# The list schedule's price of a matmul, set to other lengths

## The chip, the cores and the metric

One core of one Trainium2 chip runs the whole program. The metric is device time in microseconds (us) of one execution; lower is better. Engines: PE is TensorE, DVE is VectorE, ACT is ScalarE, POOL is GpSimd; SP issues the large loads.

## What is computed

Three transformer-like layers on one sequence of 512 tokens of width 1024, in float32. The first block mixes sparse top-k attention with a chunked state-space scan and then runs a two-of-sixteen mixture of experts. The second block runs twice; each time it does a hybrid mixer, a cross-attention to a memory of 256 rows and a SwiGLU:

```python
def first_block(x, ...):
    proj = x @ w_in                       # q, k, v, index heads, z, xbc, dt
    att  = dsa_attention(q, k, v, iq, ik, iw, topk)
    ssd  = ssd_mixer(z, xbc, dt_raw, ...)
    x = layer_norm(ALPHA * x + concat([att, ssd]) @ w_out)
    return layer_norm(ALPHA * x + hier_moe(x, ...))

def second_block(h, mem, ...):            # for each of two layers
    h = layer_norm(A2 * h + hybrid_mixer(h, ...))       # attention + RG-LRU
    h = layer_norm(A2 * h + cross_attention(h, mem, ...))
    return layer_norm(A2 * h + swiglu(h, wi, wo))       # widths 1024 -> 2816 -> 1024
```

## The kernel before, in words

**The arithmetic.** Every large product is made of three matmuls: each float32 operand is split into a high part and a low part of type float32r, and high x high, low x high and high x low are added in PSUM (`feat_mm` L850, `tok_mm` L860). The stationary tile has 128 x 128 elements, the moving one up to 512 columns. A piece of weights is loaded by SP as `raw`, cast by ACT to `wh`, and the rest `wl = raw - wh` is made by DVE, or by POOL for four keys, the first memory projection `ck0` among them (`Stream.take` L545, L572). Four pieces fit in the ring. A few small products in the state-space chunks (`ssd_chunk` L1098) and twelve warm-up matmuls are true four-byte float32 matmuls; BF16 appears in the routing alone.

**What sets the order.** Nothing is issued while the code is being read. `Plan.new` (L216) writes each instruction down with its operands, a price in ns and a priority, which is its place in the code. `Plan.run` (L349) then plays the program through: every engine is free or busy by the prices, an instruction becomes ready when the prices of what it needs have passed plus a latency between engines (`LAT`, L181), and a free engine takes the ready one that comes first in the code (`pick`, L413). The instruction is issued in that order, and on the chip each engine's queue keeps that order, whatever the real times are. A loaded tile must have a free slot before its first instruction may be taken (`held`, L399). Prices so touch neither the instructions nor their number, only their order on each queue.

**Where that leaves a choice.** In the wide products PE has one stream of ready matmuls and takes them in code order. In four stretches it has two: a chain of small steps between PE, DVE, ACT and POOL, and matmuls of low priority that cover the chain. They are the first block's chunks (`ssd_chunk`, `topk`, `attend`, L1262), covered by the memory projections `ck` and `cv` of the second block; the routing (`route` L1475), covered by more of `ck`; the experts (L1719); and the layer norms (`tok_phase` L1359, `norm_feat` L1301), covered by the first units of the next product (`feat_units` L1811). A chunk's chain ends in the inverse square root on DVE (`rsqrt` L1038, tiles `rs_y`), the scaling of `y` (L1163), and PE's transposes of `y` (L1166).

**The prices.** `Plan.add` (L306) sets them. For PE (L324 to L331) `n` is the number of output columns, `args[1]` the stationary tile and `args[2]` the moving one.

Of the kernel before, what the change touches and what calls it, by code (L numbers as in the profile page):

```python
# [14 lines left out]
BF16 = mybir.dt.bfloat16  # L15
# [177 lines left out]
class Plan:  # L193
# [112 lines left out]
    def add(self, eng, method, args, kw):  # L306
        if self.direct:
            f = lambda x: x.real() if isinstance(x, View) else x
            return getattr(eng.real, method)(*[f(x) for x in args], **{k: f(x) for k, x in kw.items()})
        views = [v for v in list(args) + list(kw.values()) if isinstance(v, View)]  # L310
        writes = [kw[k] for k in ("out", "accum_out") if isinstance(kw.get(k), View)]
        if args and "out" not in kw and isinstance(args[0], View):
            writes.append(args[0])
        reads = [v for v in views if not any(v is w for w in writes)]
        def fn():
            f = lambda x: x.real() if isinstance(x, View) else x
            return getattr(eng.real, method)(*[f(x) for x in args], **{k: f(x) for k, x in kw.items()})  # L317
        n = max([v.columns() for v in views if method in ("tensor_reduce", "max", "bn_stats") or v in writes] or [1])
        lat, table, nbytes = 0.0, None, 0
        if method == "dma_start":  # L320
            o = writes[0] if writes else reads[0]
            nbytes = o.columns() * 4 * (o.box[0][1] - o.box[0][0])
            cost = 1040.0 if eng.name == "Pool" else 60.0
        elif eng.name == "PE":  # L324
            n = writes[0].columns()
            if method == "transpose":
                cost = 109.0
            elif args[1].buf.dtype == F32:
                cost = max(216.0, 1.667 * n)
            else:  # L330
                cost = max(27.0 if args[2].buf.dtype == BF16 else 109.0, 0.4167 * n + 2.5)  # L331
        elif eng.name == "ACT":
            aps = sum(isinstance(kw.get(k), View) for k in ("bias", "scale"))
            cost = 0.836 * n + (50, 143, 235)[aps] + (0 if args[1].buf.pool.psum else 42) + (93 if "accum_out" in kw else 0)
            table = SETS.get(args[2].name)
        elif eng.name == "DVE":
            rate = 1.042
            if method in ("tensor_copy", "memset", "tensor_scalar") and not any(v.buf.pool.psum for v in views):
                rate = 0.6
            if method == "reciprocal":  # L340
                rate = 8.3
            cost = rate * n + 66 + 30 * sum(v.columns() == 1 for v in reads if n > 100)
        else:
            cost = 1.85 * n + 60
        op = self.new(eng.name, fn, cost, reads, writes, lat)
        op.table, op.bytes, op.name = table, nbytes, method
        return op
# [1934 lines left out]
```

## Time and profile before

| | us |
|---|---|
| median of 3 runs | 2419.61 (2418.84 to 2421.11) |
| the profiled execution, its own time | 2428.73 |
| its span, first to last instruction | 2426.9 |
| around the span | 1.83 |
| PE busy | 2365.1 (97%) |
| DVE, ACT, POOL busy | 1495.0, 1146.8, 359.1 |

A busy PE is not PE at its peak, since matmuls overlap in the records: their pace is read from the starts of a run of equal matmuls. The granted clock of TensorE has two levels; 1.00 in a window means the whole window at the upper one (2.4 GHz), 0.51 nearly all of it at the lower one (1.2 GHz).

### The profile page before, as it was taken

What the parts mean: (1) busy time and instruction counts of PE and PEld (TensorE: products, weight loads), DVE (VectorE), ACT (ScalarE), POOL (GpSimd) and SP (SyncE); (2) the same over time, 40 slices, a digit from 0 to 9 for tenths busy, and PEclk for the clock granted to TensorE, in tenths of its full rate; (3) what the DMA queues carried; (4) which work ended last, traced back from release to release, by engine and by line L of the source; (5) the groups of instructions that cost most, each with busy time, mean ns of one, the idle gap of its engine ahead of it and who ended that gap; (6) DMA issues with size and microseconds to landing.
All of it is one profiled execution on the core that took longest, in us unless ns stands there. A gap on an engine that the chain in (4) does not pass through costs nothing.

```text
span 2426.9 us, 30226 instructions
## 1 busy us (share of the span) xinstructions
PE 2365.1 (97%) x11681; PEld 1960.6 (81%) x11681; DVE 1495.0 (62%) x2591; ACT 1146.8 (47%) x2004; POOL 359.1 (15%) x261
## 2 busy tenths in 40 slices
PE   9999989989999999999999999999999999999998
PEld 8777877768888887888888888888887898888886
DVE  5977689986983668756333335794477756432334
ACT  5447458756762663545222235673474544322221
POOL 1462432211000004403000001000004303000000
PEclk9979999999999999999999999999999999999999
DMA  6222769984113334322222333113323322332322
GB/s 185 73 76 70 236 205 333 342 299 125 54 61 104 113 98 163 102 73 70 92 99 87 104 104 119 57 53 97 120 92 125 116 94 87 104 105 87 104 79 77
DMA packets 215426, 290.42 MB, mean 120 GB/s; under 512 B 10784, under 2 KB 166640, under 8 KB 214768
## 3 DMA queue, kind: packets, MB, share of 16 engines
q1 hardware_dynamic: 203888, 260.44, 33.0%
q0 software_dynamic: 11392, 28.02, 3.6%
q8 instruction: 92, 1.51, 0.3%
q14 instruction: 54, 0.44, 0.1%
HBM read 275.85 MB, written 20.97 MB: 122 GB/s over the span
## 4 chain that ended last, share of the span: by engine, by line
PE 76%; DVE 8%; ACT 2%; issue 1%; DMA 1%; DVEq 0%; POOL 0%; ACTq 0%; POOLq 0%
PE fu L317 10%; PE fg L317 10%; PE fo L317 10%; PE ps L317 6%; PE ba L317 4%; PE gn L317 4%; PE q L317 4%; PE xr L317 4%; PE gr L317 4%; PE ga L317 4%; PE co L317 3%; PE wo L317 3%; PE gu L317 2%; DVE hTl L317 2%; PE cq L317 2%; PE bn L317 2%
## 5 line engine op out<-in xcount | busy, mean ns | idle before, releaser
L317 DVE TENSOR_TENSOR wl<-raw,wh 128x1024 fp32r<-128x1024 f32 (+1 forms) x390 | 489.2, 1264 | 460.2 <-ACT wh L317 459.5
L317 ACT ACTIVATE wh<-raw 128x1024 fp32r<-128x1024 f32 (+1 forms) x414 | 433.8, 1057 | 551.7 <-PE fu L317 156.5
L317 POOL TENSOR_TENSOR htokL<-htokL,lngb 128x1024 f32<-128x1024 f32 x48 | 132.9, 2783 | 291.5 <-PE ps L317 288.4
L303 ACT ACTIVATE lntmp<-ps,lnc 128x128 f32<-128x128 f32 x224 | 85.3, 467 | 50.4 <-PE ps L317 38.0
L317 ACT ACTIVATE fsil<-fg 128x512 f32<-128x512 f32 x44 | 26.3, 598 | 160.1 <-PE fg L317 160.1
L317 DVE TENSOR_TENSOR fsil<-fsil,fu 128x512 f32<-128x512 f32 x44 | 30.3, 688 | 104.9 <-PE fu L317 103.4
L317 PE MATMUL fg<-hTh,wh 128*128 128x512 f32 (+1 forms) x384 | 88.2, 372 | 0.0
L317 PE MATMUL fu<-hTh,wh 128*128 128x512 f32 (+1 forms) x384 | 88.2, 372 | 0.0
L317 PE MATMUL fu<-hTl,wh 128*128 128x512 f32 (+1 forms) x384 | 88.1, 372 | 0.0
L317 PE MATMUL fg<-hTh,wl 128*128 128x512 f32 (+1 forms) x384 | 88.0, 372 | 0.0
L317 PE MATMUL fu<-hTh,wl 128*128 128x512 f32 (+1 forms) x384 | 88.0, 371 | 0.0
L317 PE MATMUL fg<-hTl,wh 128*128 128x512 f32 (+1 forms) x384 | 88.0, 371 | 0.0
L317 DVE TENSOR_TENSOR hTl<-lntmp,hTh 128x512 fp32r<-128x512 f32 x56 | 76.9, 1384 | 10.3 <-ACT hTh L317 10.2
L317 PEld LDWEIGHTS fu<-hTl,wh 128*128 128x128 f32 x384 | 68.3, 188 | 12.5
L317 PEld LDWEIGHTS fg<-hTh,wl 128*128 128x128 f32 x384 | 68.3, 188 | 12.4
L317 PEld LDWEIGHTS fg<-hTl,wh 128*128 128x128 f32 x384 | 68.3, 188 | 12.5
L317 PEld LDWEIGHTS fu<-hTh,wl 128*128 128x128 f32 x384 | 68.3, 188 | 12.5
L317 PEld LDWEIGHTS fu<-hTh,wh 128*128 128x128 f32 x384 | 68.3, 188 | 12.4
L317 PEld LDWEIGHTS fg<-hTh,wh 128*128 128x128 f32 x384 | 68.1, 188 | 12.4
L317 PE MATMUL gu<-wh,hTm 128*128 128x512 f32 x256 | 73.5, 398 | 1.2 <-DVE hl L317 1.0
L317 POOL TENSOR_TENSOR wl<-raw,wh 128x1024 fp32r<-128x1024 f32 x24 | 58.2, 2431 | 104.3 <-ACT wh L317 104.2
L317 ACT ACT_TABLE_LOAD x53 | 68.0, 1283 | 11.7 <-DVE c_mx L317 5.6
(605 smaller groups left out, 5781.6 us busy)
## 6 DMA issues: line engine op xcount, KB each, us to landing
raw<-in_w_in_dram SPq DMA_DIRECT2D x47, 1024.0 KB, 5.3
raw<-in_ffn_wi_dram SPq DMA_DIRECT2D x44, 1024.0 KB, 5.2
raw<-in_ffn_wo_dram SPq DMA_DIRECT2D x20, 1024.0 KB, 5.0
raw<-in_ckv_w_dram SPq DMA_DIRECT2D x15, 1024.0 KB, 5.4
raw<-in_w_out_dram SPq DMA_DIRECT2D x12, 1024.0 KB, 5.0
raw<-in_w_down_dram SPq DMA_DIRECT2D x8, 1024.0 KB, 7.6
raw<-in_w_br_attn_dram SPq DMA_DIRECT2D x8, 1024.0 KB, 5.0
raw<-in_w_br_rnn_dram SPq DMA_DIRECT2D x8, 1024.0 KB, 5.0
```

What stands on the lines that cost most here:

```text
L303: "ACT": (lambda: act.activation(out.real(), src.real(), AF.Identity, bias=bias.real(), scale=scale.real()), 0.836 * n + 235, 0.0)}
L317: return getattr(eng.real, method)(*[f(x) for x in args], **{k: f(x) for k, x in kw.items()})
```

## The change

Two prices of PE are set to other numbers. A matmul with a float32 stationary tile is reckoned at 1.2 ns a column, at least 112 ns, in place of 1.667 ns, at least 216 ns. Any other matmul gets 13.5 ns beside its columns in place of 2.5 ns. Transposes, latencies, loads and all prices of other engines stay.

```diff
             elif args[1].buf.dtype == F32:
-                cost = max(216.0, 1.667 * n)
+                cost = max(112.0, 1.2 * n)
             else:
-                cost = max(27.0 if args[2].buf.dtype == BF16 else 109.0, 0.4167 * n + 2.5)
+                cost = max(27.0 if args[2].buf.dtype == BF16 else 109.0, 0.4167 * n + 13.5)
```

In ns: 512 columns 215.9 before and 226.9 after; 460 columns 194.2 and 205.2; 256 columns 109.2 and 120.2; 128 columns 109 both times; float32 with 64 columns 216 and 112, with 128 columns 216 and 153.6, with 256 columns 426.8 and 307.2.

## Rows read from the trace of the kernel before

**Rows 1.** The page: busy time by engine, and the granted clock in 40 slices.
```profile
PE 2365.1 (97%) x11681; PEld 1960.6 (81%) x11681; DVE 1495.0 (62%) x2591; ACT 1146.8 (47%) x2004; POOL 359.1 (15%) x261
...
PEclk9979999999999999999999999999999999999999
```

**Rows 2.** Busy time by window: PE, PEld, DVE, ACT, POOL (instructions); clock, DMA share, GB/s.
```profile
140.00:181.00 41.00, 37.06 (x181) 29.07 (x181) 27.82 (x86) 18.10 (x55) 21.89 (x17) 0.67 0.19 63
181.00:285.00 104.00, 103.88 (x543) 82.50 (x542) 68.07 (x170) 59.19 (x112) 30.71 (x32) 1.00 0.47 148
285.00:345.00 60.00, 48.86 (x341) 42.90 (x340) 51.17 (x93) 33.37 (x70) 33.55 (x20) 0.94 0.60 195
345.00:520.00 175.00, 163.40 (x869) 131.98 (x868) 158.40 (x211) 129.26 (x176) 46.62 (x47) 0.99 0.92 311
...
560.00:2427.00 1867.00, 1842.26 (x8898) 1533.36 (x8896) 1045.44 (x1721) 811.51 (x1423) 168.70 (x100) 1.00 0.30 95
```

**Rows 3.** What PE waited for: us in total, times, longest us.
```profile
PE route L317 <- DVE hTl L317: 8.0, 3, 4.4
PE hidT L317 <- DVE sg L317: 5.8, 7, 1.2
PE ps L317 <- DVE htokL L317: 5.7, 4, 2.6
PE bn L317 <- DVE L0sg L317: 4.5, 1, 4.5
```

**Rows 4.** The chain that ended last, in order of time: start, us, what.
```profile
1128.89 2.88 PE fu L317 x24
...
1192.28 5.44 PE fu L317 x24
```

**Rows 5.** The tile ssd: durations in ns (min/median/max), first and last start.
```profile
L317 PE MATMUL ssd<-xdt,L x64: 221/275/476, 138.3 to 223.9; 128*128 128x64 f32 x64
```

**Rows 6.** PE in order of time, a chunk's four-byte matmuls.
```profile
198.20 1.10 PE L317 MATMUL ssd<-xdt,L 128*128 128x64 f32 x8
199.24 0.65 PE L317 MATMUL ssd<-xe,btk 128*64 128x256 f32 x2
```

**Rows 7.** Busy time of PE in matmuls of ck, in 141.2 to 157.2 and 303 to 338.
```profile
141.20:157.20 16.00, 9.74 (x57) 0.87 0.25 84
303.00:338.00 35.00, 18.38 (x126) 0.90 0.68 232
```

**Rows 8.** The same of cq before a layer norm's last transposes, and of fg.
```profile
996.00:1003.00 7.00, 5.03 (x40) 1.00 0.01 2
...
1118.00:1122.00 4.00, 3.11 (x24) 1.00 0.00 0
```

**Rows 9.** All engines in order of time, 150.6 to 157.3.
```profile
150.59 1.05 ACT L317 ACTIVATE wh<-raw 128x1024 fp32r<-128x1024 f32 x1
...
151.72 4.83 POOL L317 TENSOR_TENSOR wl<-raw,wh 128x1024 fp32r<-128x1024 f32 x2 [3.64 <-ACT wh L317]
151.76 1.09 ACT L317 ACTIVATE pth<-ps 128x512 fp32r<-128x512 f32 x2
151.89 2.25 DVE L317 SCALAR_TENSOR_TENSOR rs_y<-rs_e,rs_y 128x1 f32<-128x1 f32 x1
...
154.40 2.70 DVE L317 SCALAR_TENSOR_TENSOR y<-y,rs_y,nw 128x512 f32<-128x512 f32 x1
...
157.24 0.45 PE L317 MATMUL ssd<-ca,y 128*128 128x128 f32 x1 [2.69 <-DVE y L317]
```

**Rows 10.** The tile rs_y: durations in ns (min/median/max).
```profile
L317 DVE SCALAR_TENSOR_TENSOR rs_y<-rs_e,rs_y x12: 141/154/2248, 150.2 to 232.5; 128x1 f32<-128x1 f32 x12
...
L317 DVE SCALAR_TENSOR_TENSOR y<-y,rs_y,nw x4: 741/752/2698, 154.4 to 233.6; 128x512 f32<-128x512 f32 x4
```

**Rows 11.** Busy time by window again, around the fall of the clock.
```profile
157.30:181.00 23.70, 23.70 (x86) 16.82 (x87) 10.62 (x36) 7.88 (x23) 10.15 (x10) 0.51 0.14 45
181.00:235.00 54.00, 53.88 (x310) 41.38 (x309) 41.22 (x127) 36.24 (x79) 18.23 (x16) 1.00 0.21 72
```

## The prediction, made before the changed kernel was built

> **What bounds the kernel now.** I read the page first. PE is busy for 97% of the span and its clock is at the upper level in all but a few early slices [rows 1]. So the time is PE's work, which the change leaves alone, plus what PE loses to waits and to the lower clock. The windows say where that is [rows 2]. From 560 us to the end PE is busy for 1842.26 of 1867 us at clock 1.00: there the products stand one behind the other. The losses lie ahead of that: 140 to 181 us (clock 0.67), 285 to 345 us (PE idle for 11.1 of 60 us) and the experts from 345 to 520 us (idle for 11.6 of 175 us). The waits name the releasers [rows 3], and in these rows it is always DVE that is late: for the routing's transposed input, for the experts' hidden tile, for a layer norm, for a bank of `bn`.
>
> **Is the new price right?** 24 matmuls of 512 columns take 5.44 us on the chain, 226.7 ns each; 24 of 256 columns take 2.88 us, 120 ns each [rows 4]. The new 226.9 and 120.2 ns are these lengths; the old 215.9 and 109.2 ns were 5% and 9% short. The Trainium skill, "TensorE: Matmul & The Clock Gate", section "Back-to-back issue gap", gives N/2.4 + 2.5 ns for a warm 512-column matmul, about 216 ns, which is the old price. This trace disagrees by 11 ns; were the page right here, every cover below would be planned thinner than it really is by another 2.7 us in all, and the sum would come to -3.1 in place of -5.8.
>
> For the four-byte matmuls the price gets worse. The code asks for 32 products of 64 columns (eight heads, four chunks), and the trace has 64 records of them [rows 5], so one product is two records. Eight records, four products, take 1.04 us from the first start to the next tile's [rows 6], 260 ns each. The old price was 216, the new one is 112: the length of a record, not of a product. With 32 of these, twenty other products and the twelve of the warm-up, and the same work running on PE before and after, I cost this at nothing on PE; it makes the planner expect the end of a chunk's eight products 0.83 us too soon (8 x 104 ns), which can leave DVE waiting for them in the four chunks, beside PE's covering work.
>
> **What the change does, part by part.** It removes and adds no instruction and no transfer. It re-draws the order of every queue, PE's, DVE's, ACT's, POOL's and SP's.
>
> (a) Stretches with one ready stream, 560 us to the end. The order is that of the code at either price, and what covers DVE and ACT there is PE itself (1842 busy us against 1045 and 812). I cost it at 0. The wait for `bn` (4.5 us [rows 3], and its like in the second layer) stays: DVE is slow there while POOL scales the norm's rows, which no price knows of. Bounds: -2 to +2 us, under half of one `bn` wait, because a tie between two DVE instructions may fall the other way.
>
> (b) Experts, 345 to 520 us. The transfers are busy for 0.92 of it at 311 GB/s, the most of any window [rows 2]. A PE wait that went away would meet the weights' arrival. Cost 0; bounds -3 to +3 us, half of the hidden tile's 5.8 us [rows 3].
>
> (c) Thinner cover. While a chain runs through DVE, the planner fills PE with matmuls until, by its prices, the chain is back. Priced 11 ns short, the fill lasted longer on the chip than planned, and this hid some of DVE's lateness. At the right price it holds fewer matmuls and the same lateness shows by that much more. Counting the fills ahead of waits: 57 `ck` in 141.2 to 157.2 us (0.63 us) and 126 `ck` around the routing [rows 7], of which I take half, since the later ones follow the last long wait (0.69 us); 40 `cq` ahead of a layer norm's last transposes and 24 `fg` ahead of the next one [rows 8], once in each layer (0.88 and 0.53 us). Sum **+2.7 us**. Bounds 0 (no chain is late) and +5.4 us (each at the lower clock).
>
> (d) The stall at 157 us. DVE's chain for the first chunk meets two POOL subtractions that start at 151.72: one 128 x 1 instruction, begun 0.17 us later, takes 2.25 us where the median of twelve is 0.154, and the scaling of `y` takes 2.70 us where the median is 0.752 [rows 9, 10]. PE waits 2.69 us for it, and the clock is then at 0.51 for 23.7 us. PE starts 86 matmuls there, and 310 in the 54 us after it at clock 1.00 [rows 11]: at that pace 86 take 15.0 us, so 8.7 us are lost to the clock and gaps, **11.4 us** with the wait. The mix of widths differs, so this is an estimate. Whether the collision stays hangs on a margin of 0.17 us. ACT makes the `wh` that POOL subtracts from just ahead of two copies of 1.09 us together [rows 9]. With a ring slot freed 0.63 us later in the plan (57 x 11 ns) and the chunk's products ended 0.83 us sooner, the two may swap; POOL would start 1.09 us later and find the small instructions done. Bounds: -11.4 (all of it) to +11.4 us (a second one in another chunk; the old stays). I take the share of the wait that the blocked small instruction makes, 2.10 of 2.69 or 0.78, less a little for the scaling of `y`, which may still collide: three quarters, **-8.5 us**.
>
> (e) Routing, 285 to 345 us. Its waits (4.4 us the longest) are DVE's under POOL's norm rows; the order of DVE's critical steps is kept by priority. Beyond (c) 0; bounds -5 to +5 us, about the longest wait.
>
> Sum: +2.7 - 8.5 = **-5.8 us**. The profiled execution would go from 2428.73 to 2422.9 us; it stands 9.1 us (0.4%) above the median of the runs. Against the median the same sum gives **2413.8 us**, 0.24% faster. A measurement of this kernel can tell about 0.2%, 4.8 us, from no change, so the forecast lies close to that edge.
>
> **The rivals.**
>
> *No change that can be told* (2414.8 to 2424.5 us). For it: PE's work is 97% of the span, 1867 us of it have one order, and the two large terms have opposite signs. If the collision of (d) only moves (saving the 2.1 us of one blocked instruction, the clock falling all the same), the sum is +2.7 - 2.1 = +0.6, 2420.2 us. Against it: the order in the first 560 us is re-drawn as a whole, and there a single wait cost 11 us. That the change doesn't do what it says, since prices only matter where two instructions are ready together, also ends here.
>
> *Slower: a thin cover brings the clock down in another chunk.* The place is 181 to 285 us, where PE is now busy for 103.88 of 104 us at clock 1.00 with `ck` and `cv` as cover. The price of four-byte products there is too low and the cover is thinner, so transposes of `y` are queued ahead of cover that PE could have run. It decides from the point at which the granted clock falls after the wait: the wait itself is 2.7 us, the spell at the lower clock up to 8.7. With (c) and with the old stall in place: 2419.6 + 2.7 + 2.7 = 2425.0 us without the fall, 2433.7 us with all of it; in the middle 2429.4 us. For it: the waits are late DVE work, which a right price of PE does not make earlier. Against it: there the subtractions for `cv` are DVE's own, not POOL's, so DVE's small steps meet POOL less.
>
> *More than forecast.* All of (d) goes and the routing gains 5 us: -11.4 + 2.7 - 5 = -13.7, 2405.9 us. It is the low part of the forecast's case.
>
> **How the numbers follow.** Faster than 2414.8 us (the forecast, centre 2413.8, its own range 2403 to 2414.8): 0.39. No change that can be told: 0.31. Slower than 2424.5 us: 0.30. The range reaches down past the 2405.9 us of the best case by the 3 us that the experts may add, to 2403 us, and up into the slower rival to 2431 us, which leaves out its upper end. Cases of both signs hold the chance, so it is wide.
>
> **What would show it right or wrong.** (a): from the fence on, the same order of PE's units, the pace 5.44 us for 24, and `bn` waiting 4.5 us. (b): experts within 3 us of 175. (c): about 36 `cq` where 40 stand, and that wait longer by 0.4 us. (d): no `rs_y` above 1 us, and the clock of 140 to 181 us near 1.00; if the collision stands there unchanged, the forecast's main term is wrong. A clock under 0.9 in 181 to 285 us would be the slower rival. If the stretch after 560 us differs by more than 2 us, (a) is wrong, and prices matter where I hold that they don't.

## The result, and the profile after

| | before | changed |
|---|---|---|
| median of the runs, us | 2419.23 (2418.49 to 2421.11, 4 runs) | 2455.68 (2447.98 to 2456.2, 4 runs) |
| ratio | | 1.014, 95% interval 1.012 to 1.016 |
| profiled execution, its span | 2418.0 (a second profile of the same kernel) | 2453.6 |

The change costs 36 us, where the forecast was a gain of 6 with 2431 us as the upper end of its range. The spans are compared with a second profile of the kernel before, since the first [rows 1 to 11] is 9 us longer than that kernel's median: its granted clock stayed low for 24 us after the stall of [rows 9], and in the second for 3.5 us after the same stall.

The page of the changed kernel, busy time and clock, to be read against [rows 1]:

```profile
PE 2369.8 (97%) x11681; PEld 1960.4 (80%) x11681; DVE 1498.3 (61%) x2590; ACT 1147.7 (47%) x2005; POOL 351.1 (14%) x261
...
PEclk9989999999999999999999999999998999999999
```

PE has the same 11681 matmuls and still 97% of the span. The page hides a loss of this kind, because a busy PE at half clock counts as busy. Its hints are the two 8s in the row of the clock, in the third slice (the first block's chunks) and in the 31st, far behind the experts; the second profile of the kernel before has 9 in all forty slices.

DVE has one instruction less than in [rows 1] and ACT one more: prices move more than the order on each queue. `Plan.copy` (L282) gives a copy to ACT or DVE, whichever the plan has free first, and of the 32 copies `of` in the attention 18 are on ACT in place of 14. This does not explain the time of that stage: the run price_8_0 below has 24 of them on ACT, and its attention takes as long as before (126.1 us).

The windows of the changed kernel that answer to [rows 2]:

```profile
140.00:181.00 41.00, 36.60 (x216) 31.37 (x213) 31.01 (x91) 19.06 (x56) 26.12 (x20) 0.79 0.15 45
181.00:285.00 104.00, 101.36 (x534) 80.17 (x533) 68.98 (x170) 56.33 (x111) 28.42 (x30) 1.00 0.47 145
285.00:345.00 60.00, 47.03 (x282) 39.76 (x281) 46.57 (x82) 33.45 (x67) 35.85 (x18) 0.89 0.62 204
345.00:520.00 175.00, 162.88 (x907) 132.97 (x907) 157.74 (x222) 128.87 (x174) 41.30 (x46) 0.99 0.90 307
560.00:2427.00 1867.00, 1840.31 (x8896) 1528.10 (x8897) 1035.88 (x1697) 820.83 (x1446) 168.87 (x106) 0.99 0.29 95
```

Fixed windows hold other work in each kernel once they are shifted against each other. The better cut is by stage, from the first matmul of one tile to the first of another. Windows cut so, first of the second profile of the kernel before (from `xbc` to the first `ssd`, on to the first `kv`, and the attention from `ga` to `ba`), then of the changed kernel; columns as in [rows 2]:

```profile
35.10:126.60 91.50, 89.68 (x427) 71.39 (x425) 81.27 (x209) 45.89 (x78) 32.27 (x16) 1.00 0.26 81
126.60:537.60 411.00, 380.17 (x2130) 309.76 (x2128) 340.83 (x619) 262.36 (x447) 145.49 (x123) 0.98 0.67 229
...
603.70:729.80 126.10, 125.78 (x666) 103.76 (x665) 103.53 (x318) 84.03 (x219) 0.00 (x0) 1.00 0.20 63
```

```profile
35.00:130.30 95.30, 92.41 (x427) 73.77 (x425) 85.17 (x213) 45.85 (x78) 31.79 (x16) 0.98 0.25 78
130.30:555.30 425.00, 387.20 (x2131) 315.73 (x2129) 339.08 (x615) 261.48 (x441) 142.29 (x123) 0.96 0.65 219
...
622.70:750.80 128.10, 127.28 (x668) 103.72 (x667) 102.12 (x316) 84.31 (x221) 0.00 (x0) 1.00 0.20 62
```

Now the counts agree: 427 matmuls in both, 2130 and 2131, 666 and 668. The same work takes 3.8, 14.0 and 2.0 us more. Of the 14.0, half is idle PE (30.8 to 37.8 us) and half is busy time, at a clock of 0.96 in place of 0.98: 34.1 us at the lower level in place of 17.1. The largest spell is in the first block's chunks:

```profile
143.40:157.10 13.70, 13.70 (x65) 12.25 (x65) 10.68 (x42) 6.71 (x24) 7.99 (x6) 0.50 0.06 21
```

The attention stage stands once in each layer. Of its 2.0 us only 0.5 is idle PE; the rest is busy PE at a clock of 1.00 in both kernels, and what lengthens that part is not shown. With the `bn` stage of layer 1, which is 10.1 us longer up to the first `fg` (230.6 against 220.5), these come to 31.8 of the 35.6 us between the spans (3.8 + 14.0 + 2.0 + 1.9 + 10.1); the other stages add at most 1.3 each.

The waits of PE in the changed kernel, to be read against [rows 3]:

```profile
PE bn L317 <- DVE L1sg L317: 13.8, 1, 13.8
PE hidT L317 <- DVE sg L317: 10.3, 12, 1.8
PE ps L317 <- DVE htokb L317: 8.7, 3, 6.0
PE ps L317 <- DVE htokL L317: 6.8, 4, 2.9
PE kv L317 <- ACT hTh L317: 4.4, 2, 4.2
PE pos L317 <- DVE Moh L317: 4.1, 1, 4.1
PE bn L317 <- DVE L0sg L317: 3.7, 2, 3.0
```

The three routing waits of 8.0 us together are gone. In their place stand 8.7 for the first block's norm rows `htokb`, 4.1 for `pos`, and one of 13.8 in a place where the kernel before waits 4.5.

**The wait of 13.8 us.** DVE, POOL and one line of PE in order of time, changed kernel, layer 1's `bn` stage:

```profile
1863.62 0.69 DVE L317 TENSOR_TENSOR L1sg<-L1sg,L1m1t 128x512 f32<-128x512 f32 x1
...
1864.23 20.06 DVE L317 TENSOR_TENSOR wl<-raw,wh 128x1024 fp32r<-128x1024 f32 x1
...
1864.61 18.59 POOL L317 TENSOR_TENSOR htokL<-htokL,lngb 128x1024 f32<-128x1024 f32 x8
...
1884.21 0.67 DVE L317 SCALAR_TENSOR_TENSOR L1sg<-L1sg,bn 128x512 f32<-128x512 f32 x1
...
1885.03 1.19 PE L317 MATMUL bn<-L1yh,wh 128*128 128x512 f32 x2 [13.77 <-DVE L1sg L317]
```

One subtraction of DVE, otherwise 1.22 us, lasts 20.06, to the end of POOL's eight scalings, which meanwhile run undisturbed (18.59 / 8 = 2.32 us each). PE runs out of banks behind it, and the clock is at 0.50 from 1874.0 to 1891.1 us. In the kernel before, the same eight take 23.41 us, and DVE's instructions get their turn between them; those with both inputs in SBUF take 2.3 to 3.4 us each (layer 0 of its first profile; layer 1 is alike):

```profile
913.05 1.22 DVE L317 TENSOR_TENSOR wl<-raw,wh 128x1024 fp32r<-128x1024 f32 x1
...
913.81 23.41 POOL L317 TENSOR_TENSOR htokL<-htokL,lngb 128x1024 f32<-128x1024 f32 x8 [0.61 <-DMA lngb<-in_ln_g_dram]
...
917.01 2.91 DVE L317 TENSOR_TENSOR L0sg<-L0sg,L0m1t 128x512 f32<-128x512 f32 x1
```

**The wait of 6.0 us.** ACT, DVE and PE in order of time: the changed kernel, then the second profile of before, from the norm's statistics to PE's transposes.

```profile
286.04 0.21 DVE L317 BATCH_NORM_AGGREGATE lnmv<-ln 128x2 f32<-128x12 f32 x1
...
287.44 2.01 ACT L317 ACTIVATE wh<-raw 128x1024 fp32r<-128x1024 f32 x2 [18.93 <-DMA raw<-in_ckv_w_dram]
...
290.32 2.00 ACT L317 ACTIVATE wh<-raw 128x1024 fp32r<-128x1024 f32 x2 [0.88 <-DMA raw<-in_ckv_w_dram]
292.34 1.28 ACT L317 ACT_TABLE_LOAD   x1
293.63 0.29 ACT L317 ACTIVATE lnsd<-lnmv,eps 128x1 f32<-128x1 f32 x1
...
296.17 1.12 PE L317 MATMUL ps<-ca,htokb 128*128 128x128 f32 x4 [6.02 <-DVE htokb L317]
```

```profile
272.51 2.01 ACT L317 ACTIVATE wh<-raw 128x1024 fp32r<-128x1024 f32 x2 [19.37 <-DMA raw<-in_ckv_w_dram]
275.54 0.21 DVE L317 BATCH_NORM_AGGREGATE lnmv<-ln 128x2 f32<-128x12 f32 x1
275.96 2.01 ACT L317 ACTIVATE wh<-raw 128x1024 fp32r<-128x1024 f32 x2 [1.43 <-DMA raw<-in_ckv_w_dram]
...
279.28 0.29 ACT L317 ACTIVATE lnsd<-lnmv,eps 128x1 f32<-128x1 f32 x1
...
281.38 1.09 PE L317 MATMUL ps<-ca,htokb 128*128 128x128 f32 x8 [1.26 <-DVE htokb L317]
```

The root `lnsd` of the norm is queued on ACT behind four casts of weights, and the casts wait for a transfer. In the changed kernel the transfer lands 1.4 us after the statistics are ready (287.44 against 286.04); in the kernel before the first pair of casts runs 3 us ahead of them. From statistics to root it is 7.6 us in place of 3.7. The plan's order put the root there, and the landing, which no price of PE describes, made it late. It is not one execution's: in the four profiles with this order of the first block (the change and the runs after_rows_dve, after_later and new_price_first below) the root comes 6.9 to 7.8 us after the statistics and the wait is 5.4 to 6.2 us; in the four with the order of before (its two profiles, before_rows_dve and new_price_later) 3.7 to 4.0 us and 1.4 to 2.0 us.

### The profile page after: what moved, and what is told of

It is laid out like the page before. It is cut to its first block, busy times and chain, and to the rows that moved or that the text cites. A ratio compares the mean times of both kernels' runs of the same rounds, so it can differ in the third digit from the quotient of the medians.

```text
span 2453.6 us, 30245 instructions
## 1 busy us (share of the span) xinstructions
PE 2369.8 (97%) x11681; PEld 1960.4 (80%) x11681; DVE 1498.3 (61%) x2590; ACT 1147.7 (47%) x2005; POOL 351.1 (14%) x261
## 4 chain that ended last, share of the span: by engine, by line
PE 70%; DVE 7%; ACT 1%; issue 0%; DVEq 0%
PE fu L317 10%; PE fg L317 10%; PE fo L317 10%; PE ps L317 5%; PE ba L317 4%; PE gr L317 4%; PE gn L317 4%; PE xr L317 4%; PE cq L317 3%; PE q L317 3%; PE co L317 3%; PE wo L317 3%; PE ga L317 3%; PE bn L317 2%; PE gate L317 2%; DVE hTl L317 2%
## 5 line engine op out<-in xcount | busy, mean ns | idle before, releaser
L317 DVE TENSOR_TENSOR wl<-raw,wh 128x1024 fp32r<-128x1024 f32 (+1 forms) x390 | 500.5, 1294 | 472.9 <-ACT wh L317 471.3
L317 PEld LDWEIGHTS fg<-hTl,wh 128*128 128x128 f32 x384 | 68.4, 188 | 12.5
L317 PEld LDWEIGHTS fg<-hTh,wl 128*128 128x128 f32 x384 | 68.3, 188 | 12.5
L317 PEld LDWEIGHTS fu<-hTh,wl 128*128 128x128 f32 x384 | 68.3, 188 | 12.5
L317 PEld LDWEIGHTS fu<-hTh,wh 128*128 128x128 f32 x384 | 68.3, 188 | 12.5
```

## The experiments

Two theories went into the first runs. Theory A: any other price draws another order, and what DVE then meets on POOL (or ACT on a transfer) decides. Theory B: the dearer matmul makes every cover thinner, and the time grows with the price. The stages, in us, from the first matmul of one tile to the first of the next (columns: first `xbc` to first `ssd`; `ssd` to the first `kv`; attention of one layer; `bn` to `fg` in layers 0 and 1), each from the kernel's profiled execution:

| kernel | median | xbc-ssd | ssd-kv | attention | bn-fg 0 | bn-fg 1 |
|---|---|---|---|---|---|---|
| before, first profile | 2419.61 | 91.5 | 420.5 | 126.1 | 221.2 | 220.9 |
| before, second profile | 2423.16 | 91.4 | 411.1 | 126.1 | 220.4 | 220.5 |
| only_four_byte | 2416.67 | 91.5 | 411.6 | 126.2 | 221.4 | 220.8 |
| price_minus_8_5 | 2436.82 | 89.5 | 419.8 | 125.0 | 220.1 | 227.4 |
| price_3_5 | 2415.63 | 91.4 | 413.7 | 125.3 | 221.1 | 220.8 |
| price_8_0 | 2440.85 | 93.6 | 427.1 | 126.1 | 221.9 | 220.4 |
| price_12_5 | 2448.64 | 92.6 | 420.9 | 127.8 | 221.8 | 231.4 |
| only_13_5 | 2446.83 | 95.3 | 425.8 | 128.1 | 221.1 | 231.4 |
| the change | 2455.68 | 95.3 | 425.0 | 128.0 | 221.1 | 230.6 |
| price_24_5 | 2476.94 | 101.2 | 427.2 | 131.4 | 222.7 | 223.0 |
| after_half_rows | 2450.81 | 95.2 | 429.5 | 128.1 | 217.9 | 231.4 |
| after_later | 2446.13 | 95.3 | 426.4 | 128.1 | 222.1 | 220.6 |
| late_400 | 2445.44 | 93.1 | 423.9 | 126.9 | 221.0 | 231.2 |
| new_price_first | 2437.54 | 94.4 | 428.0 | 126.1 | 221.0 | 221.0 |
| new_price_later | 2437.68 | 91.4 | 409.3 | 128.1 | 221.5 | 220.9 |
| after_rows_dve | 2433.75 | 94.2 | 428.5 | 128.0 | 215.4 | 215.4 |
| before_rows_dve | 2406.66 | 91.5 | 411.1 | 126.2 | 214.6 | 214.6 |
| four_rows_dve | 2406.1 | 91.5 | 406.8 | 126.2 | 214.7 | 214.8 |
| p3_5_rows_dve | 2401.35 | 91.4 | 411.7 | 125.2 | 214.8 | 213.3 |
| four_3_5_rows_dve | 2408.26 | 91.4 | 419.1 | 125.2 | 214.5 | 214.7 |

Each row of stages is one execution, and executions of one order differ. The four profiles with the first block's order of before have 91.4 to 91.5 and 409.3 to 420.5 us in the first two columns, the four with that of the change 94.2 to 95.3 and 425.0 to 428.5. So the order costs time in both stages, but a difference under some 11 us in `ssd-kv` between two single profiles can be the execution's.

**before_again**: the kernel before, unedited.

> The kernel before, once more, with a second profile. Its first profiled execution took 2428.7 us and its timed runs 2419.2. If single executions differ by where DVE's instructions fall among POOL's (both theories allow it), this profile is near 2419 and one of the three marked stretches is shorter: 140 to 181 us (clock 0.67 before) or the bn wait of layer 0 or 1 (4.5 us each, about 7 us with the clock). If the order alone fixes the time, the same stretches show the same losses within 1 us.

Measured: ratio 1.0004 (0.9989 to 1.0019), runs from 2419.75 to 2430.18 us. The stall of the first chunk is in this profile too:

```profile
154.37 2.26 DVE L317 SCALAR_TENSOR_TENSOR rs_y<-rs_e,rs_y 128x1 f32<-128x1 f32 x1
...
157.77 0.44 PE L317 MATMUL ssd<-ca,y 128*128 128x128 f32 x1 [3.88 <-DVE y L317]
```

```profile
157.00:160.50 3.50, 2.73 (x9) 2.38 (x10) 2.51 (x4) 0.60 (x1) 1.14 (x2) 0.53 0.69 167
140.00:181.00 41.00, 35.55 (x246) 29.77 (x245) 33.78 (x104) 24.76 (x70) 23.19 (x17) 0.96 0.24 77
```

The wait is 3.9 us, longer than the 2.7 of [rows 9], but the clock is low for 3.5 us only, and 140 to 181 us has 0.96 where [rows 2] show 0.67. So the long spell at the lower clock is not in every execution of the kernel. Two of these ten runs took some 2430 us and may hold it; no trace shows them.

**only_four_byte** and **only_13_5**: one price of the change each, the other left as it was.

```diff
-                cost = max(216.0, 1.667 * n)
+                cost = max(112.0, 1.2 * n)
```

```diff
-                cost = max(27.0 if args[2].buf.dtype == BF16 else 109.0, 0.4167 * n + 2.5)
+                cost = max(27.0 if args[2].buf.dtype == BF16 else 109.0, 0.4167 * n + 13.5)
```

> Only the price of the four-byte matmuls is changed (112 ns or 1.2 ns a column; the others keep 2.5 ns). Theory A (the order of the first 560 us is drawn anew by any change of a price, and what DVE's instructions then meet on POOL decides): off the 2419 us by several us either way, most likely 2415 to 2435. Theory B (thinner cover in proportion to the price): the four-byte price adds no cover and takes none, so 2419 within 4 us. If the four-byte price is the fault itself, about 2440 to 2455.

> Only the 13.5 ns in place of 2.5; the four-byte price as before. Theory A: some time between 2415 and 2460, with the front part (start of layer 0's first gate unit, 611.5 us before, 622.7 after) and the bn waits unlike both. Theory B: the whole of the loss, 2448 to 2456, with the front part near 622.

Measured: 0.9986 (0.9969 to 1.0003) and 1.0093 (1.0062 to 1.0125). The float32 price by itself costs nothing, as forecast; the 13.5 ns carry most of the loss. only_13_5's profiled execution, at 2458.33 us, has the same stages as the change, the held instruction in layer 1 (20.11 us) included. Its other four took 2444.27 to 2447.4 us, so its median is 9 us below the change's. That fits an instruction that is held in some executions only, but no trace of the shorter ones shows it, and whether the float32 price adds to the 13.5 ns stays open.

**after_half_rows**: the change, with POOL's scalings of rows cut into halves of 512 columns.

```diff
-            e.tensor_tensor(htok[t], htok[t], gb[0], op=OP.mult)
-            e.tensor_tensor(htok[t], htok[t], gb[1], op=OP.add)
+            for c in (slice(0, 512), slice(512, 1024)):
+                e.tensor_tensor(htok[t][:, c], htok[t][:, c], gb[0][:, c], op=OP.mult)
+                e.tensor_tensor(htok[t][:, c], htok[t][:, c], gb[1][:, c], op=OP.add)
```

> The changed kernel with POOL's scaling of the norm's rows cut into halves of 512 columns (same elements, twice as many instructions). Theory A: the one DVE subtraction of 20.06 us in layer 1's bn stage is a meeting of DVE with POOL's burst of eight; with other lengths the meeting falls otherwise, no DVE instruction there over 6 us, bn wait of layer 1 below 6 us in place of 13.9, time 2438 to 2448. Theory B (the order of the queues makes the bn wait): the order there is the same but for POOL, so the wait stays near 14 us and the time near 2455.

Measured: 1.0103 (1.007 to 1.0137), 2450.81 us. Layer 1 of this kernel, in order of time:

```profile
1864.31 21.25 DVE L317 TENSOR_TENSOR wl<-raw,wh 128x1024 fp32r<-128x1024 f32 x1
1864.77 19.69 POOL L317 TENSOR_TENSOR htokL<-htokL,lngb 128x512 f32<-128x512 f32 x16
```

Theory A had expected no instruction over 6 us there, and was wrong: sixteen instructions of half the length hold DVE as eight did. It is the burst that holds it, not one long instruction.

**price_minus_8_5, price_8_0, price_24_5**: other prices beside the columns, the old float32 price (`+ 2.5` becomes `- 8.5`, `+ 8.0`, `+ 24.5`).

> The price 0.4167 n - 8.5 ns (22 ns under the true length at 512 columns; 256 columns meet the floor of 109), four-byte price as before: covers planned thicker than before. Theory B (thin cover: the time grows with the price): 2405 to 2419, at or below the kernel before, with layer 0's first gate unit at or ahead of 604 us. Theory A (each price draws another order, and what DVE meets on POOL decides): not ordered by the price, anything from 2415 to 2460.

> The price 0.4167 n + 8.0 ns, half way between the two kernels, four-byte price as before. Theory B: half of the loss, 2428 to 2438, layer 0's first gate unit near 613. Theory A: not half way but in one place for each meeting: layer 1's bn wait either about 4.6 or about 14 us, nothing between, and the front part anywhere from 600 to 625.

> The price 0.4167 n + 24.5 ns, 11 ns over the true length, four-byte price as before: covers planned thinner still. Theory B: as far again beyond 13.5, 2465 to 2480, layer 0's first gate unit near 640. Theory A: no further growth with the price, 2420 to 2460.

Measured: 1.0061 (1.0032 to 1.009), 1.0072 (1.0045 to 1.0099) and 1.0216 (1.0179 to 1.0254). The old 2.5 ns is ahead of this lower price and of these higher ones. The table parts the two theories by stage. In `xbc-ssd` and the attention, theory B has the direction: 89.5 to 101.2 and 125.0 to 131.4 us from the lowest price to the highest, if not at every step. In `ssd-kv` the whole does not follow the price: 427.1 at 8.0 ns, 420.9 at 12.5, 427.2 at 24.5. Its idle PE does, roughly: 29.2 us at -8.5 ns, 30.8 at 2.5 (second profile), 31.8 at 8.0, 35.9 at 12.5, 37.1 in only_13_5 and 39.8 at 24.5. What scatters is the time at the lower clock: 17.1 us at 2.5 ns, 54.6 at 8.0, 30.7 at 12.5, 31.5 at 24.5. Of the 54.6 at 8.0 ns, 27.3 are one spell, like that of 24 us in the first profile of before. price_24_5's profile is of its shortest execution, 2464.93 us; the other three took 2476.16 to 2478.7.

**late_400**: the change, with 400 ns more planned latency from ACT and DVE to PE, which puts cover back.

```diff
-LAT = {"PEACT": 197, "PEDVE": 197, "PEPool": 222, "PEPE": 0, "ACTACT": 153, "ACTDVE": 142, "ACTPE": 271, "ACTPool": 180,
-       "DVEDVE": 127, "DVEACT": 128, "DVEPE": 202, "DVEPool": 153, "PoolPE": 203, "PoolPool": 120}
+LAT = {"PEACT": 197, "PEDVE": 197, "PEPool": 222, "PEPE": 0, "ACTACT": 153, "ACTDVE": 142, "ACTPE": 671, "ACTPool": 180,
+       "DVEDVE": 127, "DVEACT": 128, "DVEPE": 602, "DVEPool": 153, "PoolPE": 203, "PoolPool": 120}
```

> The changed kernel (13.5 ns and the four-byte price) with the planner's latency from ACT and from DVE to PE longer by 400 ns, so that covers are thick again although the price is true. Theory B: most of the front part's loss comes back: layer 0's first gate unit from 622.7 to 604 to 612, time 2425 to 2440 (the bn wait of layer 1 may stay). Theory A: no tie between the latency and the time, 2415 to 2460, with a bn wait of 4.6 or 14.

Measured: 1.0081 (1.005 to 1.0113). `xbc-ssd` falls from 95.3 to 93.1 us and the attention from 128.0 to 126.9 in each layer. So putting cover back returns 2.2 + 2 x 1.1 = 4.4 of the 7.7 us lost there, as thin cover asks for. Some 1 us of the 2.2 is within what the profiles of the change's order differ by. Of the whole, theory B had expected 2425 to 2440 us, and missed: `ssd-kv` (423.9, with 41.7 us of idle PE) and the held instruction (20.14 us) stay.

**after_rows_dve, before_rows_dve, four_rows_dve**: `load_rows` (L2096) scales on DVE, in the change, in the kernel before, and with the float32 price alone.

```diff
-                    norm_rows(t, gb, G)
+                    norm_rows(t, gb, V)
```

> The changed kernel, with the eight layer-norm scalings of load_rows in each layer moved from POOL to DVE, so that no burst of POOL runs beside the bn stage. Theory A (the loss in layer 1's bn stage is DVE held up by POOL's burst): no DVE operation there takes over 4 us, both stages from the first bn projection to wo come to 44 to 46 us (before: 51 to 52; changed: 50.6 and 61.5), and the run to 2432 to 2438 us, that is 2455 less 5 to 7 and less 15 to 17. Rival (the new order itself makes PE wait there, whoever scales the rows): layer 1's stage stays near 61 us, and the run at 2448 to 2456.

> The kernel before, with the same move of the row scalings from POOL to DVE. Theory A: POOL's burst slows DVE to half its pace there too, and is what the 4.5-us wait of bn comes from: 6 to 7 us less in each layer, 2405 to 2410 us. Rival (the wait is set by the weights' landing or by DVE's own work, which gets longer by the eight scalings): no gain, or up to 5 us lost, 2418 to 2430.

> Only the four-byte price of the change, the old 2.5 ns for all matmuls, and the row scalings on DVE: the candidate to beat both kernels. Theory A: only_four_byte's 2416.7 less 6 to 7 us in each layer, 2402 to 2408. Rival as for before_rows_dve: 2416 to 2428.

Measured: 1.0053 (1.0036 to 1.007), 0.9946 (0.9929 to 0.9962) and 0.9948 (0.9929 to 0.9966); 2433.75, 2406.66 and 2406.1 us. The additions `L1sg + L1m1t` of layer 1, minimum, median and longest in ns, in the second profile of before and in before_rows_dve:

```profile
L317 DVE TENSOR_TENSOR L1sg<-L1sg,L1m1t x8: 679/692/2906, 1838.3 to 1876.4; 128x512 f32<-128x512 f32 x8
```

```profile
L317 DVE TENSOR_TENSOR L1sg<-L1sg,L1m1t x8: 682/684/692, 1831.5 to 1864.4; 128x512 f32<-128x512 f32 x8
```

Without the burst no instruction is slowed, although DVE has eight more, and the two layers gain 5.8 and 5.9 us in the kernel before (220.4 and 220.5 to 214.6) and 5.7 and 15.2 in the change. The rival, that the new order itself makes PE wait there, is out, the more so by the next run, which leaves the scalings on POOL. That the stage up to `wo` came to 33.6 us in before_rows_dve, where 44 to 46 had been expected of the changed kernel (and came, 44.8), only moves work across that border: `wo` to `fg` took 181.0 there.

**after_later**: the change, with one small load more on POOL's queue, which starts the burst later against DVE.

```diff
+                later = lnp.tile([P, KT], F32, name="later")
+                G.dma_start(later, gbs[0].rearrange("(k p) -> p k", p=P))
                 gb = load_gb(*gbs)
```

> The changed kernel with one small DMA more on POOL's queue ahead of the load of the layer norm's gain, which shifts POOL's burst against DVE by about 0.9 us and changes nothing of the work beside it. Theory A in its narrow form (DVE is held for the whole burst when the burst starts within half a microsecond after a DVE instruction's start): DVE's operations in layer 1's bn stage are 2.8 to 2.9 us each, as in the kernel before, the stage from bn to wo is 51 to 53 us, and the run 2444 to 2447. Rival (the burst holds DVE in this order wherever it starts): an operation of 19 to 21 us is there again, the stage is near 61 us, the run 2453 to 2457.

Measured: 1.0106 (1.0089 to 1.0123), 2446.13 us, as theory A had it. Layer 1, in order of time:

```profile
1865.54 1.22 DVE L317 TENSOR_TENSOR wl<-raw,wh 128x1024 fp32r<-128x1024 f32 x1
...
1867.27 2.30 DVE L317 SCALAR_TENSOR_TENSOR hTl<-L1sg,hTh 128x512 fp32r<-128x512 f32 x1
1869.50 2.90 DVE L317 TENSOR_TENSOR L1sg<-L1sg,L1m1t 128x512 f32<-128x512 f32 x1
```

The burst starts 0.76 us after the subtraction, and DVE's instructions alternate with it as before. An added load shortens the stage by 10.0 us (`bn` to `fg` 230.6 to 220.6).

**new_price_first, new_price_later**: both new prices only ahead of the fence behind the experts (L1771), or only behind it (there `self.late == True`).

```diff
+                cost = max(112.0, 1.2 * n) if self.late == False else max(216.0, 1.667 * n)
...
+                cost = max(27.0 if args[2].buf.dtype == BF16 else 109.0, 0.4167 * n + (13.5 if self.late == False else 2.5))
...
         plan.fence(further)
+        plan.late = True
```

> The two new prices for all that is written ahead of the fence after the experts (the first block and its cover), the old ones behind it. Theory A (the loss is made of stages that add up): xbc to ssd 95 us (before 91.5), ssd to the second block's first kv 425 (before 411), every later stage as before within 1 us, and no long DVE operation in either bn stage: 2421 + 4 + 14 = 2439 us, 2434 to 2444. Rival (the first block's order changes what the later stages meet): a held DVE operation in layer 1 again, 2446 to 2452.

> The old prices ahead of the fence, the two new ones for all behind it. Theory A: first block as before, the attention stages 128 us each (before 126.1), bn to wo of layer 1 at 61 us with one DVE operation of 19 to 21 us, since the order behind the fence is the changed kernel's: 2421 + 1 + 2 x 2.5 + 10 = 2437 us, 2432 to 2440. By the prediction's step (a), that prices do nothing behind the experts: 2419 to 2423.

Measured: 2437.54 us, 1.0073 (1.0056 to 1.0091), and 2437.68, 1.0075 (1.0056 to 1.0095). Each half of the change loses some 17 us, together nearly the whole. The later half's profiled execution is its fastest, 2427.65 us, with no held instruction; its other three took 2435.37 to 2440.59. The 8 to 13 us between fit an instruction that is held in some executions and not in others, though no trace of the longer ones shows it.

**price_3_5, price_12_5**: 1 ns from the old price and from the new.

> Old price of float32 matmuls, 3.5 ns beside the columns in place of 2.5. Theory A (any other order meets other work): xbc to ssd and the attention stages as before within 0.5 us, but ssd to kv anywhere from 411 to 430 us: 2421 to 2441, and 10 more with a held operation in bn. Theory B (the time grows with the price, from 2421 at 2.5 ns to 2447 at 13.5, 2.3 us per ns): 2422 to 2425.

> Old price of float32 matmuls, 12.5 ns beside the columns, 1 less than the change has. Theory B: 2.3 us below only_13_5's 2446.8, 2443 to 2446. Theory A: xbc to ssd 95 and attention 128 us as at 13.5, ssd to kv 411 to 430, layer 1's bn stage 51 or 61 us: anywhere from 2428 to 2450, as likely outside 2443 to 2446 as in it.

Measured: 0.9975 (0.9964 to 0.9987), 2415.63 us, and 1.0114 (1.0096 to 1.0131), 2448.64 us. At 3.5 ns both theories had asked for 2421 us or more, and the kernel got faster than before. At 12.5 ns theory B asked for less than the 2446.83 us of 13.5, and it did not come; the two can't be told apart. Theory A's free choice of 411 to 430 in `ssd-kv` is too loose as well: the profiles with 2.5 or 3.5 ns in the first block stand at 406.8 to 420.5, with 411.6 in the middle of nine, those with -8.5 or 8 ns and more at 419.8 to 429.5, with 426.4 in the middle of eleven.

**p3_5_rows_dve, four_3_5_rows_dve**: what the runs found, put together: 3.5 ns and the rows on DVE, with the old float32 price and with the changed one.

> 3.5 ns beside the columns, the old float32 price, row scalings on DVE. If the two gains add: price_3_5's 2415.6 less the 14 that the row scalings gave before_rows_dve, 2401 to 2403 us, ssd to kv as in price_3_5 (414) and attention 125.3 us in both layers. If the move of the scalings disturbs the first block: 2405 to 2412.

> The same with the change's float32 price. Theory A (the first block's time belongs to the order drawn and not to the price): attention 125.3 us as in price_3_5, but ssd to kv anywhere from 407 to 428, so 2395 to 2417 us. If 3.5 ns is the better price by itself: within 3 us of p3_5_rows_dve.

Measured: 0.9923 (0.991 to 0.9937), 2401.35 us, and 0.9955 (0.9942 to 0.9969), 2408.26 us. The two gains add, and p3_5_rows_dve beats both kernels: 19 us ahead of the one before, some 54 ahead of the changed one. The float32 price, worth nothing by itself, costs 7 us here by the medians. The profiles put it into `ssd-kv` (419.1 against 411.7), as theory A has it, though single executions differ there by as much.

## Why the prediction was wrong, step by step

**Is the new price right?** Yes as a length; the last chain of the changed kernel still steps by 5.44 us for 24 matmuls of 512 columns. But a truer price did not make a better order: 2.5 or 3.5 ns, too short by 11 or 10, gave the best times. A likely reason, which no run shows by itself, is that the prices play against latencies and landings in the plan that are not true. The Trainium skill, "TensorE: Matmul & The Clock Gate", section "Back-to-back issue gap", calls its 216 ns the gap of an isolated matmul and gives 131 ns for a sustained stream of 512 columns. This trace agrees with neither: its runs of 24 take 227 ns each. The prediction's two sums, -5.8 by the trace and -3.1 by the page, both had the wrong sign.

**Float32 matmuls cost nothing**: right by themselves (0.9986), but not in every order: 7 us between p3_5_rows_dve and four_3_5_rows_dve.

**(a) One stream from 560 us on, 0, bounds -2 to +2**: this step failed most plainly. From the first `kv` on the changed kernel is 17.9 us longer, and new_price_later has the new prices only there and loses 17 us by its median. Two things were wrong. The attention stages run with a second stream and cost 2.0 and 1.9 us; the text counted four stretches with a choice and took the attention for none. And the `bn` wait was bounded by half of itself, "because a tie between two DVE instructions may fall the other way": the step named the cause, POOL scaling the rows, and took the pace of [rows 3] (4.5 us) for the worst it could do. It did 13.8.

**(b) Experts, 0, bounds -3 to +3**: right in size. From the first `gu` to the first `kv` it is 197.5 us against 194.9, and the hidden tile's waits rose from 5.8 to 10.3 us.

**(c) Thinner cover, +2.7, 0 to +5.4**: the mechanism was right as far as the runs show it, the size off. At the place where it was counted it came as worked out. PE before the last transposes of layer 0's norm:

```profile
1012.48 0.76 PE L317 MATMUL cq<-hTh,wl 128*128 128x256 f32 x5
1016.15 1.09 PE L317 MATMUL ps<-ca,htokL 128*128 128x128 f32 x8 [2.91 <-DVE htokL L317]
```

With the four groups of eight ahead of them these make 37 `cq` where 40 stood [rows 8], and the wait is 2.9 us in place of 2.6. The four waits of this kind come to 6.8 us in place of 5.7. The missed terms are `xbc-ssd` (3.8 us) and the attention (3.9 in both layers), where cover is laid between short steps many times over. In the kernel before neither has a wait over 0.9 us, so neither was in the rows of waits that the count began from. late_400 gave back up to 4.4 of these 7.7 us.

**(d) The stall at 157 us, -8.5**: the term that gave the sum its sign, and it failed. Most of it was the 8.7 us of clock beside the wait, which are not in every execution: the profiled one stood 9.1 us above the median, and the prediction took them off the median all the same. In the second profile the lower level lasts 3.4 us there. The wait for `y` did go, from 3.9 us to 0.2, but 2.3 us for `sm` stand in the same chunk, and the slowed small instructions are still there. The clock did not come near 1.00 either: 140 to 181 us has 0.79, with 13.7 us at the lower level from 143.4 us on. All four profiles with this order of the first block have that spell, so it belongs to the order; what starts it is not worked out. The tile `rs_y` in the changed kernel (minimum, median, longest in ns):

```profile
L317 DVE SCALAR_TENSOR_TENSOR rs_e<-rs_y,rs_w x12: 205/216/2411, 155.9 to 233.6; 128x1 f32<-128x1 f32 x12
L317 DVE SCALAR_TENSOR_TENSOR rs_y<-rs_e,rs_y x12: 145/159/2253, 158.6 to 233.8; 128x1 f32<-128x1 f32 x12
```

**(e) Routing, 0, bounds -5 to +5**: the order of DVE's critical steps did keep, but for a few, and the routing waits went. What came in their place was on ACT's queue, the root behind casts behind a transfer (6.0 us), and `pos` (4.1, though between 1.1 and 4.1 in the four profiles of this order). The whole of `ssd-kv` is 14.0 us longer, where (b), (d) and (e) had come to -8.5 together. Half of it is idle time, of which these two waits are the largest single parts, half the lower clock, more than half of that in the chunks of (d). Why orders drawn at 2.5 or 3.5 ns are mostly shorter there than those of the other prices is not settled; no run took away ACT's casts or the landings.

**The rivals.** The slower one had the sign and not the place: 181 to 285 us kept its clock of 1.00 and lost 2.5 us of PE (103.88 to 101.36). A fall of the clock in the chunks did come, but ahead of that place, from 143.4 us on; the one collision more came in a stage taken for settled. No change was ruled out by the interval.

## What to carry to other kernels

A list schedule's prices are not improved one at a time: set one to its true length, and margins that may have stood in for others (latency, late transfers, a slowed engine) go with it; so compare a price at both neighbours before believing in it. Where two engines collide in a plan that does not know of it, take the collision away (here eight scalings a layer moved to the other engine, 14 us in the kernel before) rather than rely on an order that happens to miss it. Bound a known collision by the length of the whole burst, not by the wait it causes today. And before a loss in one profile is taken off a median, ask whether the median holds it: a second profile of the same kernel told.

## What the runs showed of the hardware that was not expected

A DVE subtraction with both inputs in SBUF was held for 19 to 21 us, through all of POOL's eight (or sixteen shorter) instructions, in six profiles. In all six POOL's first instruction started 0.05 to 0.47 us after the held one, and took 2.4 us (1.3 for a half), its undisturbed length. Where DVE's instruction had started 0.53 us or more ahead, it was never held. That is not the whole rule: ahead of five other bursts such an instruction had started 0.10 to 0.45 us before and was not held either, while POOL's first instruction took 2.7 to 3.1 us. What decides between them is not seen. The instructions that read one input from PSUM (`L1sg<-L1sg,bn`) took 0.68 us beside the same bursts.

The Trainium skill, "SBUF — State Buffer", section "Who interferes with whom", says that a DVE instruction with two SBUF inputs contends with a GpSimd instruction that reads SBUF, and that one with at most one SBUF input, outside the modes that use both ports, does not; these rows agree. Its rule that issue order decides who blocks does not cover this case: the held instruction is recorded as started first, by 0.38 us in the changed kernel, and it waited for eight instructions and not for one.
